# Four reorderings in a two-layer encoder kernel: transposes, operand combinations, a tanh, and a last combination

## The chip, the cores and the metric

The kernel runs on one core of a Trainium2 chip. The metric is the device time of one execution in microseconds, the median of several runs. The names of the engines are those of the profile: PE multiplies matrices, DVE is the vector engine, ACT the scalar engine (copies and activation functions), POOL and SP mainly issue DMAs here.

## What is computed

The reference is an encoder trunk on 512 tokens of width 1024, in float32, with two layers and a final RMSNorm:

```python
for l in range(DEPTH):
    x = x + 0.5 * swiglu(rms_norm(x, ffn1_norm[l]), ffn1_w_in[l], ffn1_w_out[l])
    x = x + mixer(rms_norm(x, mix_norm[l]), ...)
    x = x + 0.5 * swiglu(rms_norm(x, ffn2_norm[l]), ffn2_w_in[l], ffn2_w_out[l])
return rms_norm(x, final_norm)

def mixer(h, w_in, gate_bias, rpb, w_na_out, w_f_out, w_o):
    ...
    y_na = neighbourhood_attention(q, k, v, rpb) @ w_na_out
    y_f = fourier_mix(uf) @ w_f_out
    g_na = jax.nn.sigmoid(ga + gate_bias[0])
    g_f = jax.nn.sigmoid(gf + gate_bias[1])
    return (g_na * y_na + g_f * y_f) @ w_o
```

SwiGLU has width 2816. The weights come from HBM, some blocks more than once; the trace shows 355 MB read.

## The kernel before

**Arithmetic.** Every float32 operand is split into a rounded part hi and a remainder lo; ACT makes hi (L286, or L172 for a negated weight) and DVE makes lo (L287, or L173). A product is then three matmuls, hi·hi, hi·lo and lo·hi (`mm3`, L280 to L282), each 128x128 by 128x512. Activations are the stationary operand, weights the moving one.

**Strassen.** The large matrix products are done on 2x2 blocks in seven products instead of eight. `product` takes one of them: four k-tiles by two token blocks by three matmuls, 24 in all, into a pair of PSUM banks. The operands are blocks of the activations or combinations of them; in the gate blocks t1, t2 and t3 (`minus`, L1078 and L1079, the additions at L1087, then `parts`, which splits them into t1h, t1l and so on). Pair A holds products 1, 6, 7 and 4 in turn, pair B products 5 and 3, pair C product 2. Before a pair gets its next product, `snap` (L436, ACT) copies it out as sn.

**Weights.** `Stream` holds the list of weight granules (128x1024, 512 KB) in the order of use. `ws.next()` hands out the next one and sees to it that two more are split; raw granules are fetched up to eight ahead, by DMAs from SP (L150). Sums of two weight blocks come from additive DMAs that POOL issues (L152 at loading, L179 after a granule has been split) or from DVE (L170). There are three buffers for hi and three for lo of a granule, so the split of one has to wait until the matmuls of the granule three places earlier are through.

**Order.** The kernel is written in a tile framework. The program text gives a priority, and a scheduler plans the queue of each engine, with buffers taken from rotating pools (23 slots of 4 KB per partition in the main one, eight PSUM banks); on the chip each engine then works its queue off. So two instructions of one engine can stand in another order than in the text. `tc.high_priority()` puts the small steps of `rstd` first.

**The places that the change touches.**

- FFN stage (`stage_ffn`): the first 256 columns are done plainly (pairs `pcl`, four banks), then five column blocks `jb` by Strassen. The plain block's gate is tanh (L510, needs `norm.rh` from `rstd`) and two DVE steps per half (L514, L515); its result is transposed by `to_at` (PE L459, ACT L463). The loop's order of products is 1, 5, 6, 2, 7, 3, 4. Behind it come the 21 steps of the output matrix, with `make` for the operand of a step (DVE L546, split into c1h, c1l and so on), three steps for product 4 at the end; c4 is their operand. In the last FFN `finish` multiplies the finished half of x by its rstd and the final gain (L662) and stores it.
- Mixer (`stage_mixer`): after attention and Fourier mixing, `fill(o, ns, 0)` multiplies the attention output by half of `na_w_out` (n: four token blocks of 12 matmuls, copied out at L933 as fs). Then two gate blocks, one for each half of the 1024 channels, with products in the order 1, 5, 2, 6, 7, 3, 4; `after` names functions to call behind a product. Behind the products `less` (L441), `arg` (L944, tanh at L948) and `gated` (L952) make the gates; `both` (L959) adds the two branches. The first block's result `ga0` = fs[0, j], j being the half of the tokens, is transposed by `to_channels` (PE L1023, ACT L1024) into mq, the operand of the output matrix `w`, whose first operands m1 and m5 are read behind the second gate block.
- `squares` (L322): ACT squares x, keeps the row sums, and writes the squares themselves into a scratch tile, junk.

Of the kernel before, what the change touches and what calls it, by code (L numbers as in the profile page):

```python
# [9 lines left out]
F32 = mybir.dt.float32  # L10
F32R = mybir.dt.float32r
BF16 = mybir.dt.bfloat16
I32 = mybir.dt.int32
AF = mybir.ActivationFunctionType
ALU = mybir.AluOpType
AX = mybir.AxisListType

P = 128
D = 1024
T = 512  # L20
# [72 lines left out]
def encoder_kernel(  # L93
# [3 lines left out]
    V, S, G, PE = nc.vector, nc.scalar, nc.gpsimd, nc.tensor  # L97

    cp = ctx.enter_context(tc.tile_pool(name="cp", bufs=1))
    sp = ctx.enter_context(tc.tile_pool(name="sp", bufs=1))  # L100
# [8 lines left out]
    def nm(s):  # L109
        uid[0] += 1  # L110
        return f"{s}_{uid[0]}"

    def slot(dt=F32, s="k", shape=(4, 256)):
        return kp.tile([P, *shape], dt, tag="k", name=nm(s), bufs=23)
# [8 lines left out]
    def pair(s="ps"):  # L123
        return [bank(s), bank(s)]
# [119 lines left out]
    class Stream:  # L244
# [25 lines left out]
        def next(self):  # L270
            self.prep(self.pos + 1 + AHEAD)
            it = self.items[self.pos]
            self.pos += 1
            return it.out

    ws = Stream()
# [29 lines left out]
    class Norm:  # L306
# [10 lines left out]

        def squares(self, i, j):
            for tb in (2 * j, 2 * j + 1):
                junk = sp.tile([P, T], BF16, tag="junk", name=nm("junk"), bufs=1)  # L320
                k = 4 * i + tb
                S.activation(junk, x[:, tb, i * T : (i + 1) * T], AF.Square, accum_out=self.ssq[:, k : k + 1])  # L322

# [102 lines left out]
    def parts(src, s):  # L426
        h, l = slot(F32R, s + "h"), slot(F32R, s + "l")
        split(h, l, src)
        return h, l, 0
# [3 lines left out]
    def snap(ps):  # L433
        t = slot(F32, "sn", (2, T))
        for b in range(2):
            S.activation(t[:, b, :], ps[b], AF.Copy)  # L436
        return t
# [5 lines left out]
    def stage_ffn(norm, nxt, late):  # L443
# [25 lines left out]
        pcl = [pair("cl"), pair("cl")]  # L469
# [20 lines left out]
        for js in ((1,), (0,)):  # L490
# [4 lines left out]
        t1 = combo(b11, b11, b12, ALU.subtract, "t1")  # L495
        t3 = combo(b12, b12, b22, ALU.subtract, "t3")
        t2 = combo(b22, b22, b11, ALU.add, "t2")
# [3 lines left out]
        acts = {  # L501
            1: (hx[0], lx[0], 0), 2: (hx[1], lx[1], 0), 3: (hx[1], lx[1], 256), 4: (hx[0], lx[0], 256),
            5: t1, 6: t2, 7: t3,
        }
        late_at = []
        for j in range(2):
            th = slot(F32, "th", (2, 256))
            for b in range(2):
                c = 2 * j + b
                S.activation(th[:, b, :], pcl[j][b][:, 0:256], AF.Tanh, scale=norm.rh[:, c : c + 1])  # L510
            for b in range(2):
                c = 2 * j + b
                g, u = pcl[j][b][:, 0:256], pcl[j][b][:, 256:512]
                V.scalar_tensor_tensor(th[:, b, :], th[:, b, :], 1.0, g, ALU.add, ALU.mult)  # L514
                V.scalar_tensor_tensor(th[:, b, :], u, norm.r2[:, c : c + 1], th[:, b, :], ALU.mult, ALU.mult)  # L515
            late_at.append((th, j, 0, 2))

        def settle_at():
            while late_at:
                to_at(*late_at.pop(0))  # L520
# [52 lines left out]
        for jb in range(NB):  # L573
            f0 = 2 + 4 * jb
            pa = pair("A")
            product(pa, acts[1], K4, True)
            s1 = snap(pa)
            if jb:
                settle_at()
            pb = pair("B")  # L580
            product(pb, acts[5], K4, True)
            sb = snap(pb)
            settle_at()
            product(pa, acts[6], K4, False, again=True)
            s2 = snap(pa)
            pc = pair("C")
            product(pc, acts[2], K4, True)
            less(pc, s1)
            z1 = gate(s1, 0)
            product(pa, acts[7], K4, False, again=True)  # L590
            less(pa, sb)
            product(pb, acts[3], K4, False, again=True)
            less(pb, s2)
            z2 = gate(s2, 1)
            times(z2, [sb[:, 0, :], sb[:, 1, :]], 1)
            if jb == NB - 1:
                make(0)
                make(1)
            product(pa, acts[4], K4, False, again=True)
            times(z1, pa, 0)  # L600
            late_at += [(z2, 1, f0, 4), (z1, 0, f0, 4)]

        ps = {}
        for i, (m, c, _) in enumerate(steps):
            make(i)
            if i:
                make(i + 1)
            key = {6: 1, 4: 7}.get(m, m)
            if key not in ps:
                ps[key] = pair(f"o{key}")  # L610
            if m == 4 and c == 0 and nxt.mix:
                ws.finish_stage()
                swap_pools(1)
            product(ps[key], made.pop(i), list(range(len(CHUNK[0][c]))), c == 0 and m in (1, 2, 3, 5, 7), c == 2, m in (4, 6))
            if i == 0:
                settle_at()
            make(i + 2)
            if not late:
                if i == 6:
                    nxt.quad(0, 0)  # L620
                elif m == 4 and c == 0:
                    nxt.quad(1, 1)
                    nxt.quad(0, 1)
            if c < 2:
                continue
            if m == 1:
                update(ps[1], 0, 0, -1)
            elif m == 2:
                update(ps[2], 0, 0, 1)
                nxt.squares(0, 0)  # L630
            elif m == 5:
                update(ps[5], 0, 1, 1)
                update(ps[5], 1, 1, -1)
            elif m == 6:
                for q in ((1, 1, 1), (0, 1, -1), (1, 0, 1)):
                    update(ps[1], *q)
            elif m == 7:
                update(ps[7], 1, 1, 1)
                nxt.squares(1, 1)
            elif m == 3:  # L640
                update(ps[3], 0, 1, 1)
                nxt.squares(0, 1)
                if late:
                    finish(nxt, 1)
            else:
                update(ps[7], 1, 0, 1)
                nxt.squares(1, 0)
                if late:
                    finish(nxt, 0)
                else:  # L650
                    nxt.later((1, 0))
# [3 lines left out]
    def finish(norm, j):  # L655
        if gf[0] is None:
            gf[0] = slot(F32, "gf", (D,))
            nc.sync.dma_start(out=gf[0], in_=bass.AP(tensor=gfin.tensor, offset=gfin.offset, ap=[[0, P], [1, D]]))
        r = norm.rstd((j,))
        for b in range(2):  # L660
            o_ = slot(F32, "o", (D,))
            V.scalar_tensor_tensor(o_, x[:, 2 * j + b, :], r[:, b : b + 1], gf[0], ALU.mult, ALU.mult)  # L662
            nc.sync.dma_start(out=out[:, 2 * j + b, :], in_=o_)


    def stage_mixer(l, norm, nxt):
# [140 lines left out]
        o, q, k, bms = [], {}, {}, {}  # L807
# [116 lines left out]
        fs, ns = {}, {}  # L924

        def fill(src, to, i):

            w = [ws.next(), ws.next()]
            for tb in range(TB):
                if tb % 2 == 0:  # L930
                    to[i, tb // 2] = slot(F32, "fs", (2, T))
                ps = rows_of(src, tb, w)
                S.activation(to[i, tb // 2][:, tb % 2, :], ps, AF.Copy)  # L933
                yield
# [81 lines left out]
        def to_channels(i, ga, j):  # L1016
            mq[i, j] = slot(F32, "mq")
            for q in range(2):
                tr = bank("tr").rearrange("p (a b) -> p a b", a=2)
                for k in range(2):  # L1020
                    for b in range(2):
                        d = (2 * q + k) * P
                        PE.transpose(tr[:, k, b * P : (b + 1) * P], ga[j][:, b, d : d + P], ident)  # L1023
                S.activation(mq[i, j][:, 2 * q : 2 * q + 2, :], tr, AF.Copy)  # L1024

        u = proj_U()
# [37 lines left out]
        bias = []  # L1064
# [10 lines left out]
        def minus(p, q, s):  # L1075
            t, u = slot(F32, s), slot(F32, s)
            for z, d in enumerate((t, u)):
                V.tensor_tensor(d, p[z], q[z], ALU.subtract)  # L1078
            V.tensor_tensor(t, t, u, ALU.add)  # L1079
            return t  # L1080

        t12 = minus(B[0, 0], B[0, 1], "t1")
        acts[5] = parts(t12, "t1")
        for _ in fill(o, ns, 0):
            pass
        for z in B[1, 1]:
            V.tensor_tensor(t12, t12, z, ALU.add)  # L1087
        acts[6] = parts(t12, "t2")

        def third():  # L1090
            acts[7] = parts(minus(B[0, 1], B[1, 1], "t3"), "t3")
# [3 lines left out]
            V.tensor_tensor(t12, t12, B[1, 0][1], ALU.add)  # L1095
            split(hx[0][:, :, 256:512], lx[0][:, :, 256:512], t12)

        ga0 = gate_block(0, bias, acts, {2: third, 6: fourth})

        def turn():  # L1100
            for j in range(2):
                to_channels(0, ga0, j)

        ga1 = gate_block(1, bias, acts, {1: turn})
        m00, m01 = mq[0, 0], mq[0, 1]
        a1 = parts(m00, "m1")
        a5 = combo(m00, m00, m01, ALU.subtract, "m5")
# [71 lines left out]
    norm = Norm(0)  # L1179
# [149 lines left out]
```

## Time and profile before

| What | Value |
|---|---|
| Median of 3 runs | 1972.65 us (1972.23 to 1976.64) |
| The profiled execution itself | 1974.07 us |
| Its span, first to last instruction | 1971.8 us |
| Mean granted TensorE clock | 0.992 |
| PE matmuls | 8997 |
| DMA | 361.82 MB, 183 GB/s mean |

Times in the profile count from the start of the span. A row of a timeline has its start, its length, engine, line, operation, output<-inputs, shapes, a count, and in brackets the idle time of the engine before it and what ended that. A row of the stretches has its bounds and length, then busy time and instructions of PE, PEld (weight loads), DVE, ACT and POOL, then the granted clock of PE (1.00 is full speed), the share of the DMA engines' time that was busy, and GB/s. A row of the waits has the waiting instruction, what it waited for, the sum in us, how often, and the longest.

### The profile page before, as it was taken

The page shows a single profiled execution, that of the slowest core. Times are in us where ns is not written, and L with a number is a line of the kernel's source. Part 1 is how long each engine was busy: PE and PEld are TensorE (multiplying, and loading weights), DVE is VectorE, ACT ScalarE, POOL GpSimd, SP SyncE. Part 2 cuts the span into 40 slices and gives each one's busy share as a digit, 9 for nine tenths or more (in the row PEclk, how much of TensorE's full clock was granted, in tenths as well). Part 3 has the DMA queues.
Part 4 walks back from the last instruction along what each step waited for, and adds up shares of the span by engine and source line. Part 5 has one row for each costly group of instructions (what it writes and reads, how often), then busy time and mean ns, then how long its engine had stood idle before and what let it go on. Part 6 is the DMA issues. An engine that isn't in the chain of part 4 may idle for free.

```text
span 1971.8 us, 24577 instructions
## 1 busy us (share of the span) xinstructions
PE 1923.9 (98%) x8997; PEld 1590.0 (81%) x8997; DVE 1617.0 (82%) x1936; ACT 1122.8 (57%) x1594; POOL 199.3 (10%) x242
## 2 busy tenths in 40 slices
PE   8999999999999999999999999999999999999997
PEld 6888887888778888888788888878887788888885
DVE  8777899598779877889977878996878788777897
ACT  6555666445555655566555556653555566555653
POOL 0011011200111000101000100102101110000010
PEclk9999999999999999999999999999999999999999
DMA  8677599221977567749757765974039874775692
GB/s 291 172 193 201 154 250 328 70 67 55 256 194 200 139 185 203 188 151 261 225 139 203 190 171 171 283 254 113 28 116 238 204 192 133 207 180 161 186 282 104
DMA packets 105704, 361.82 MB, mean 183 GB/s; under 512 B 12016, under 2 KB 14192, under 8 KB 105584
## 3 DMA queue, kind: packets, MB, share of 16 engines
q1 hardware_dynamic: 78576, 266.92, 39.8%
q0 software_dynamic: 27008, 93.34, 25.9%
q8 instruction: 70, 1.15, 0.2%
q14 instruction: 50, 0.41, 0.1%
HBM read 354.97 MB, written 2.10 MB: 181 GB/s over the span
## 4 chain that ended last, share of the span: by engine, by line
PE 78%; DVE 12%; issue 3%; DMA 3%; ACT 2%; SPq 0%; DVEq 0%; ACTq 0%
PE A L280 8%; PE A L282 8%; PE A L281 8%; PE o L281 5%; PE o L282 5%; PE o L280 5%; PE B L280 4%; PE B L281 4%; PE B L282 4%; PE ps L281 4%; PE ps L282 4%; PE ps L280 4%; DVE wlo L287 3%; DMA raw<-in_wst_dram 3%; PE C L282 2%
## 5 line engine op out<-in xcount | busy, mean ns | idle before, releaser
L287 DVE TENSOR_TENSOR wlo<-raw,whi 128x1024 fp32r<-128x1024 f32 (+1 forms) x522 | 621.8, 1197 | 275.7 <-ACT whi L286 274.7
L286 ACT ACTIVATE whi<-raw 128x1024 fp32r<-128x1024 f32 (+1 forms) x522 | 540.8, 1038 | 524.2 <-PE A L282 133.2
L152 POOL DMA_DIRECT2D raw<-in_wst_dram x152 | 131.8, 877 | 1369.5 <-DMA raw<-in_wst_dram 861.4
L170 DVE TENSOR_TENSOR raw<-raw,raw 128x1024 f32<-128x1024 f32 (+1 forms) x128 | 151.0, 1189 | 2.4
L281 PE MATMUL A<-wlo,xh 128*128 128x512 f32 x384 | 149.5, 389 | 0.6 <-DVE wlo L173 0.6
L282 PE MATMUL A<-whi,xl 128*128 128x512 f32 x384 | 149.4, 389 | 0.0
L280 PE MATMUL A<-whi,xh 128*128 128x512 f32 x384 | 148.6, 389 | 0.0
L172 ACT ACTIVATE whi<-raw 128x1024 fp32r<-128x1024 f32 x76 | 78.9, 1038 | 86.5 <-PE B L282 33.2
L173 DVE SCALAR_TENSOR_TENSOR wlo<-raw,whi 128x1024 fp32r<-128x1024 f32 x76 | 89.9, 1194 | 22.0 <-ACT whi L172 22.0
L281 PEld LDWEIGHTS A<-wlo,xh 128*128 128x128 f32 x384 | 72.1, 188 | 16.0 <-DVE wlo L173 1.0
L280 PEld LDWEIGHTS A<-whi,xh 128*128 128x128 f32 x384 | 72.1, 188 | 14.9
L282 PEld LDWEIGHTS A<-whi,xl 128*128 128x128 f32 x384 | 72.1, 188 | 14.9
L436 ACT ACTIVATE sn<-A 128x512 f32<-128x512 f32 x96 | 56.9, 598 | 43.3 <-PE A L282 43.3
L280 PE MATMUL A<-whi,t3h 128*128 128x512 f32 x192 | 76.2, 397 | 4.7 <-ACT sn L436 4.7
L280 PE MATMUL A<-whi,t2h 128*128 128x512 f32 x192 | 76.0, 396 | 3.9 <-ACT sn L436 2.7
L280 PE MATMUL B<-whi,t1h 128*128 128x512 f32 x192 | 76.8, 401 | 1.1 <-ACT whi L286 1.1
L281 PE MATMUL A<-wlo,t2h 128*128 128x512 f32 x192 | 75.5, 393 | 1.5 <-DVE wlo L287 1.5
L281 PE MATMUL B<-wlo,t1h 128*128 128x512 f32 x192 | 75.3, 392 | 0.8 <-DVE wlo L287 0.8
L281 PE MATMUL A<-wlo,t3h 128*128 128x512 f32 x192 | 76.1, 396 | 0.0
L282 PE MATMUL A<-whi,t3l 128*128 128x512 f32 x192 | 75.9, 395 | 0.0
L282 PE MATMUL A<-whi,t2l 128*128 128x512 f32 x192 | 75.4, 392 | 0.0
L282 PE MATMUL B<-whi,t1l 128*128 128x512 f32 x192 | 75.1, 391 | 0.0
(336 smaller groups left out, 4930.4 us busy)
## 6 DMA issues: line engine op xcount, KB each, us to landing
raw<-in_wst_dram SPq DMA_DIRECT2D x462, 512.0 KB
raw<-in_wst_dram POOLq DMA_DIRECT2D x168, 512.0 KB, 8.0
raw<-in_wst_dram SPq DMA_DIRECT2D x32, 256.0 KB
vs<-v SPq DMA_DIRECT2D x12, 256.0 KB
bw<-in_rpb_dram SPq DMA_DIRECT2D x32, 68.0 KB
xt<-in_xtr_dram SPq DMA_DIRECT2D x8, 256.0 KB
x<-in_xin_dram SPq DMA_DIRECT2D x4, 512.0 KB
raw<-in_wst_dram POOLq DMA_DIRECT2D x8, 256.0 KB, 9.2
```

The source lines that it names most:

```text
L152: G.dma_start(out=self.t, in_=wst[GRAN_AT[self.plus]][:, 0 : self.n], accum_op=ALU.add)
L170: V.tensor_tensor(t, t, self.add.t, ALU.add)
L172: S.activation(hi, t, AF.Copy, scale=-1.0)
L173: V.scalar_tensor_tensor(lo, t, -1.0, hi.bitcast(F32), ALU.mult, ALU.subtract)
L280: PE.matmul(ps, lh, rh, start=start, stop=False, skip_group_check=again)
L281: PE.matmul(ps, lh, rl, start=False, stop=False, skip_group_check=again)
L282: PE.matmul(ps, ll, rh, start=False, stop=stop, skip_group_check=again)
L286: S.activation(hi, src, AF.Copy)
L287: V.tensor_tensor(lo, src, hi.bitcast(F32), ALU.subtract)
L436: S.activation(t[:, b, :], ps[b], AF.Copy)
```

## The change

- The transposes of `ga0` stood behind product 1 of the second gate block, both halves together (`turn`). Now half j=1 stands behind product 5 and half j=0 behind product 2.
- t1 and t2 of the gate blocks, t2 formerly behind n, are both made ahead of n, in a region that fixes the order of DVE's instructions: the splits of n's two granules and of product 1's first, t1, t2, then what `next(n_fill)` issues on DVE first, the split of product 1's second granule. Other engines are not bound by the region. t3 moves from behind product 2 to behind product 1.
- In the FFN stages with `norm.idx` 0 (the first of the program) the plain block's tanh and DVE steps move from ahead of the loop to behind the copies of products 1 and 5, and its transposes from ahead of product 6 to behind it. In the other FFN stages they stay.
- In the last FFN, `make(i + 3)`, the operand of the very last step, is called ahead of `finish` for half j=1.
- junk gets two buffers instead of one.

```diff
-                junk = sp.tile([P, T], BF16, tag="junk", name=nm("junk"), bufs=1)
+                junk = sp.tile([P, T], BF16, tag="junk", name=nm("junk"), bufs=2)
...
-        for j in range(2):
-            th = slot(F32, "th", (2, 256))
...
-            late_at.append((th, j, 0, 2))
+
+        def plain_out():
+            for j in range(2):
+                th = slot(F32, "th", (2, 256))
...
+                late_at.append((th, j, 0, 2))
+
+        if norm.idx:
+            plain_out()
...
             sb = snap(pb)
-            settle_at()
+            if jb == 0 and norm.idx == 0:
+                plain_out()
+            else:
+                settle_at()
             product(pa, acts[6], K4, False, again=True)
             s2 = snap(pa)
+            settle_at()
...
                 if late:
+                    make(i + 3)
                     finish(nxt, 1)
...
-        t12 = minus(B[0, 0], B[0, 1], "t1")
-        acts[5] = parts(t12, "t1")
-        for _ in fill(o, ns, 0):
+        with tc.manual_schedule(engines={mybir.EngineType.DVE}):
+            ws.prep(ws.pos + 3)
+            t12 = minus(B[0, 0], B[0, 1], "t1")
+            acts[5] = parts(t12, "t1")
+            for z in B[1, 1]:
+                V.tensor_tensor(t12, t12, z, ALU.add)
+            acts[6] = parts(t12, "t2")
+            n_fill = fill(o, ns, 0)
+            next(n_fill)
+        for _ in n_fill:
             pass
-        for z in B[1, 1]:
-            V.tensor_tensor(t12, t12, z, ALU.add)
-        acts[6] = parts(t12, "t2")
...
-        ga0 = gate_block(0, bias, acts, {2: third, 6: fourth})
-
-        def turn():
-            for j in range(2):
-                to_channels(0, ga0, j)
-
-        ga1 = gate_block(1, bias, acts, {1: turn})
+        ga0 = gate_block(0, bias, acts, {1: third, 6: fourth})
+
+        ga1 = gate_block(1, bias, acts, {5: lambda: to_channels(0, ga0, 1), 2: lambda: to_channels(0, ga0, 0)})
```

More of the change, by code (lines that the diff above doesn't have):

```diff
@@ L505, in stage_ffn @@
         late_at = []
-        for j in range(2):
-            th = slot(F32, "th", (2, 256))
[L508 to L515, printed above, removed]
-            late_at.append((th, j, 0, 2))
+        def plain_out():
+            for j in range(2):
+                th = slot(F32, "th", (2, 256))
+                for b in range(2):
+                    c = 2 * j + b
+                    S.activation(th[:, b, :], pcl[j][b][:, 0:256], AF.Tanh, scale=norm.rh[:, c : c + 1])
+                for b in range(2):
+                    c = 2 * j + b
+                    g, u = pcl[j][b][:, 0:256], pcl[j][b][:, 256:512]
+                    V.scalar_tensor_tensor(th[:, b, :], th[:, b, :], 1.0, g, ALU.add, ALU.mult)
+                    V.scalar_tensor_tensor(th[:, b, :], u, norm.r2[:, c : c + 1], th[:, b, :], ALU.mult, ALU.mult)
+                late_at.append((th, j, 0, 2))
+        if norm.idx:
+            plain_out()
         def settle_at():
```

## The prediction

> **What bounds the kernel now.** I read the page, then who PE waits for, then the stretches around the long waits with the granted clock, then single engines there.
>
> ```profile
> span 1971.8 us, 24577 instructions
> ...
> PE 1923.9 (98%) x8997; PEld 1590.0 (81%) x8997; DVE 1617.0 (82%) x1936; ACT 1122.8 (57%) x1594; POOL 199.3 (10%) x242
> ```
> ```profile
> PE tr L1023 <- DVE fs L959: 8.6, 2, 4.5
> PE A L280 <- ACT sn L436: 7.5, 3, 2.7
> PE o L282 <- DVE c4l L287: 4.1, 1, 4.1
> ...
> PE A L281 <- DVE wlo L287: 1.5, 2, 0.8
> ...
> PE A L280 <- ACT whi L286: 1.1, 2, 0.7
> ```
>
> PE is busy 1923.9 of 1971.8 us, so only 47.9 us are idle, and no other engine can gain anything unless PE waits for it. Five rows of its waits hold 22.8 us, and all five stand where the diff edits: L1023 are the moved transposes (once in each of two layers), L436 are the PSUM copies that tanh stands ahead of, c4l is the last combination, and the two short rows are the first gate block. Each place has its stretch:
>
> ```profile
> 43.50:54.50 11.00, 8.26 (x34) 6.56 (x34) 8.50 (x13) 7.89 (x14) 0.00 (x0) 0.84 0.32 105
> 526.00:540.00 14.00, 10.47 (x37) 7.59 (x36) 12.37 (x13) 8.62 (x10) 2.98 (x4) 0.88 0.81 196
> 557.00:567.00 10.00, 5.90 (x28) 4.91 (x27) 4.77 (x5) 4.65 (x7) 1.72 (x2) 0.83 0.86 205
> 1500.00:1514.00 14.00, 10.14 (x36) 7.35 (x35) 11.99 (x13) 8.29 (x10) 2.77 (x4) 0.88 0.79 188
> 1531.00:1541.00 10.00, 5.51 (x28) 4.73 (x27) 5.14 (x5) 4.64 (x7) 1.72 (x2) 0.83 0.95 238
> 1950.00:1960.00 10.00, 5.93 (x20) 4.40 (x19) 4.74 (x10) 0.00 (x0) 0.00 (x0) 0.83 0.26 105
> ```
> ```profile
> 961.00:969.00 8.00, 5.48 (x16) 3.77 (x15) 7.21 (x8) 4.60 (x7) 0.00 (x0) 0.79 0.74 220
> 576.00:596.00 20.00, 20.00 (x90) 16.57 (x89) 16.45 (x20) 10.90 (x12) 2.58 (x3) 1.00 0.92 218
> ```
>
> The second column is PE's busy time, the third from the end the granted clock, the next the DMA share. Two losses can be read off. Idle is length less busy: 2.74, 3.53, 4.10, 3.86, 4.49 and 4.07 us, 22.8 in all. Lost clock is length times (1 − clock): 1.8, 1.7, 1.7, 1.7, 1.7 and 1.7 us, 10.3 in all, because after such a pause matmuls run at a lower clock for a while. So at most about 33 us can be had in the four places. The last row is the undisturbed pace: 90 matmuls in 20 us, 0.22 us each, 5.3 us for a product of 24 and 2.7 for half of one (one weight granule).
>
> [...]
>
> **Part 1, the transposes of the merged half.**
>
> ```profile
> 554.21 1.21 DVE L959 TENSOR_TENSOR fs<-fs,fs 128x1024 f32<-128x1024 f32 x1
> ...
> 556.00 2.35 DVE L287 TENSOR_TENSOR wlo<-raw,whi 128x1024 fp32r<-128x1024 f32 x2
> ...
> 560.55 1.22 DVE L959 TENSOR_TENSOR fs<-fs,fs 128x1024 f32<-128x1024 f32 x1
> ```
>
> All 16 transposes stand behind the first product of the second gate block, which needs 5.3 us, and the half j=0 is added up only at 561.77. Half j=1 is ready at 555.42. After the change PE goes straight into the next product, whose weights are split by 558.35; j=1 is transposed some 5.3 us later and j=0 another 6 us later, both behind their additions. The 16 transposes and four copies (L1024) are the same work. Their readers, the first operands of the output matrix, come five products later. Gone are 4.10 + 1.7 and 4.49 + 1.7 = 12.0 us. What can be late next is a transfer: the DMA shares are 0.86 and 0.95 there. If half comes back as DMA waits it is 6. I take 11.
>
> **Part 2, the gates' combinations.** Of the 3.53 us in layer 0, 1.2 are waits for weights (whi, wlo) and 2.36 for the copy of A behind the sixth product.
>
> ```profile
> 526.48 1.06 ACT L286 ACTIVATE whi<-raw 128x1024 fp32r<-128x1024 f32 x1 [5.87 <-DMA raw<-in_wst_dram]
> 527.44 1.04 ACT L286 ACTIVATE t3h<-t 128x1024 fp32r<-128x1024 f32 x1
> ...
> 531.47 1.06 ACT L948 ACTIVATE sn<-sn 128x1024 f32<-128x1024 f32 x1 [2.04 <-DVE sn L944]
> ...
> 533.38 1.06 ACT L436 ACTIVATE sn<-A 128x512 f32<-128x512 f32 x2
> ```
> ```profile
> 580.47 0.60 ACT L436 ACTIVATE sn<-A 128x512 f32<-128x512 f32 x1
> ```
>
> The second gate block has the same copy at 580.47 and, by its row above, no idle time: one half is copied while PE finishes the other. So 2.36 us are not inherent; the copy is late because t3, less, tanh and a weight copy pile up in front. With t1, t2 and t3 out of the way all 3.53 + 1.7 can go. The price is in the first product:
>
> ```profile
> 506.87 1.06 ACT L172 ACTIVATE whi<-raw 128x1024 fp32r<-128x1024 f32 x1 [7.90 <-issue]
> 508.18 1.06 ACT L286 ACTIVATE whi<-raw 128x1024 fp32r<-128x1024 f32 x1 [0.25 <-PE ps L282]
> 509.15 1.04 ACT L286 ACTIVATE t1h<-t 128x1024 fp32r<-128x1024 f32 x1
> ```
> ```profile
> 502.54 1.22 DVE L1079 TENSOR_TENSOR t<-t,t 128x1024 f32<-128x1024 f32 x1
> 507.96 1.23 DVE L173 SCALAR_TENSOR_TENSOR wlo<-raw,whi 128x1024 fp32r<-128x1024 f32 x1 [4.20 <-ACT whi L172]
> ...
> 512.93 1.23 DVE L1087 TENSOR_TENSOR t<-t,xl 128x1024 f32<-128x1024 f32 x1
> ...
> 516.34 1.22 DVE L287 TENSOR_TENSOR t2l<-t,t2h 128x1024 fp32r<-128x1024 f32 x1
> ```
>
> n's last matmul ends just before 508.18, so the first product starts about 508 and wants the lo half of its second granule (L173, ready at 509.19) at about 510.9. The region on DVE puts that split behind t1l, two additions and t2l. Best: ACT makes t1h at once at 503.76, and 1.04 + 1.22 + 2.46 + 1.04 + 1.22 + 1.23 end at 511.97, a wait of 1.1. Worst: only DVE is pinned, t1h stays behind both weight copies until 510.19, the additions end at 514.16 as now, t2h, t2l and the split end about 517.6, a wait of 6.7. Between them: PE is handed the fifth product's ready half meanwhile and waits about 2. That PE's order is not bound to the code shows here, where transposes that the code names ahead of the product run inside it:
>
> ```profile
> 46.83 0.39 PE L282 MATMUL A<-whi,t2l 128*128 128x512 f32 x1
> 47.06 0.27 PE L459 MATMUL tr<-ident,th 128*128 128x128 f32 x1
> 47.09 0.54 PE L280 MATMUL A<-whi,t2h 128*128 128x512 f32 x1
> ```
>
> Queued behind the waiting DVE are the splits of the fifth product and the additive loads that POOL issues after them. The net of a layer lies between −5.2 + 1.1 = −4.1 and −5.2 + 6.7 + 1.7 = +3.2. I take the middle wait of 2 us and 0.7 for transfers that are late at the quicker pace (share 0.81): −2.5 a layer, −5 in all.
>
> **Part 3, tanh of the first plain block.**
>
> ```profile
> 43.21 1.06 ACT L286 ACTIVATE whi<-raw 128x1024 fp32r<-128x1024 f32 x1 [2.84 <-DVE rh L389]
> 44.17 1.55 ACT L510 ACTIVATE th<-cl,rh 128x256 f32<-128x256 f32 x4
> 45.59 1.10 ACT L436 ACTIVATE sn<-A 128x512 f32<-128x512 f32 x2
> ```
>
> The copies of A need only the first product, but stand behind four tanh that need rstd. Moved in front they fit into ACT's 2.84 us idle ahead of 43.21, and PE need not stop: the gain is up to 2.74 + 1.8 = 4.5. Against it: the four pcl banks stay taken until the tanh and eight DVE steps are through, and the eight transposes and pair C wait for them; they have the sixth product's 5.3 us as cover, and without it the wait just moves, gain 0. I take 3.5. The second junk buffer I cost at nothing: both squares are ACT's own, in order.
>
> **Part 4, the last combination.**
>
> ```profile
> 1948.37 1.04 ACT L286 ACTIVATE c4h<-at 128x1024 fp32r<-128x1024 f32 x1
> ```
> ```profile
> 1951.40 2.48 DVE L662 SCALAR_TENSOR_TENSOR o<-x,r,gf 128x1024 f32<-128x1024 f32 x2
> 1953.79 1.22 DVE L287 TENSOR_TENSOR c4l<-at,c4h 128x1024 fp32r<-128x1024 f32 x1
> ```
>
> c4h is there at 1949.41; c4l waits for the rstd steps and the two output products of 2.48 us. With c4l ahead of the products alone, PE still waits 4.07 − 2.48 = 1.6: gain 2.5, and 4.2 if the clock stays up. Ahead of the rstd steps too, nothing is left: 5.8. The output of half j=1 goes 1.2 us later, still 12 us ahead of the end. I take 4.5.
>
> **Sum.** 11 + 5 + 3.5 + 4.5 = 24 us. The profiled execution took 1974.07 us (span 1971.8, 2.3 around it), 1.4 above the median of 1972.65; the edits take the same from either, so 1972.65 − 24 = about 1949.
>
> **Rivals.** (A) The chain does not do what it says, because ACT's order is not pinned: t1h stays behind the weight copies and the first product waits 6.7 us. For it: the order of the rows 506.87 to 509.15. Against: PE can be given other products. Price +3.2 × 2 instead of −5: 1972.65 − 24 + 11.4 = about 1960. (B) All goes, 12 + 8.2 + 4.5 + 5.8 = 30.5: about 1942. For it: the second gate block runs the same pattern without idle time. Against: DMA share 0.95. (C) Transfers take the place of the waits: half of part 1 comes back and parts 2 and 3 give nothing: 24 − 5 − 5 − 3.5 = 10.5, about 1962. (D) Slower: t2h comes to stand in ACT's queue behind a weight copy that waits for its transfer, as t3h did at 526.48. The split that the first product needs would follow near 530, 19 us late; with 1.7 of clock less 5.2 that is +15.5 a layer, 31 less the other 19: about 1985. It decides from a delay of about 13 us a layer. Against: that copy needs a buffer which the first product still holds.
>
> **How the numbers follow.** Forecast 0.52, A 0.18, B 0.12, C 0.13, D 0.05. A run can tell 0.3%, about 6 us, from no change; forecast, A, B and most of C lie beyond it: faster 0.89, same 0.06, slower 0.05. The range leaves out D and the ends of B and C: 1940 to 1963. The instruction order is planned anew for the whole program, which may move waits elsewhere by a few us (the 2.5 us at 961 occur in one of four such blocks).
>
> **What would show it.** Part 1: no wait on L1023, clock 1.00 there. Part 2: copies of A at the sixth product without PE idle, and a wait for wlo L173 of 1 to 2 us (right) or 6 (A). Part 3: sn ahead of th on ACT. Part 4: c4l ahead of o. Wrong would be new PE waits for raw transfers in the gate blocks.

## The result and the profile after

The changed kernel took 1960.36 us (median of 4 runs, 1957.84 to 1960.91), the one before, in the same sitting, 1974.61 (4 runs). The ratio is 0.9926 with a 95% interval of 0.9909 to 0.9943, that is −14.25 us. The profiled execution took 1960.45 us. The forecast was −24 us to 1949, rival (A) said 1960. In this kernel the moved lines lie 10 lower in the mixer and in the last combination's surroundings (L1023 is L1033, L1087 is L1097, L662 is L672), and the tanh L510 is L512.

The page of the kernel after, span and busy time:

```profile
span 1958.0 us, 24573 instructions
...
PE 1918.9 (98%) x8997; PEld 1585.9 (81%) x8997; DVE 1616.4 (83%) x1936; ACT 1121.0 (57%) x1594; POOL 198.3 (10%) x242
```

Idle time of PE is 1958.0 − 1918.9 = 39.1 us, against 47.9 before. The view of PE's waits in the kernel after tells which are left:

```profile
PE A L281 <- DVE wlo L173: 12.4, 4, 5.7
PE o L281 <- DVE wlo L287: 4.5, 5, 1.6
...
PE A L281 <- DVE wlo L287: 0.5, 1, 0.5
```

The waits of the transposes, of the copies of A and of c4l are gone from the list. A new one heads it: product 1 of the first gate block waits for the split of its second granule, 5.7 us in each layer. The stretches of the kernel after at the same places:

```profile
39.50:50.50 11.00, 10.61 (x49) 8.28 (x49) 10.42 (x18) 8.82 (x16) 0.00 (x0) 1.00 0.53 147
505.00:519.00 14.00, 8.27 (x28) 6.37 (x27) 11.48 (x10) 6.80 (x11) 3.41 (x4) 0.76 0.85 201
528.00:542.00 14.00, 14.00 (x63) 11.37 (x62) 8.77 (x10) 7.11 (x8) 2.61 (x3) 1.00 0.91 226
548.00:572.00 24.00, 23.60 (x111) 19.11 (x110) 19.97 (x23) 14.39 (x18) 4.86 (x6) 1.00 0.97 233
1476.00:1492.00 16.00, 10.27 (x33) 7.88 (x33) 13.19 (x12) 7.79 (x11) 3.41 (x4) 0.79 0.91 222
1518.00:1542.00 24.00, 24.00 (x115) 20.05 (x115) 19.77 (x22) 14.68 (x19) 5.16 (x6) 1.00 0.94 233
1926.00:1942.00 16.00, 14.38 (x61) 11.02 (x60) 15.73 (x24) 10.83 (x17) 0.00 (x0) 1.00 0.00 1
```

Four of the places look as forecast. The first FFN (39.5) is down from 2.74 us idle to 0.39, at full clock. Behind product 6 of the first gate block (528) PE has no idle time. The transposes (548 and 1518) have 0.40 and 0.00 us, at clock 1.00. At the end (1926) 1.62 us are left of 4.07. The two rows of clock 0.76 and 0.79 are new: 14.00 − 8.27 = 5.73 us and 16.00 − 10.27 = 5.73 us of idle time, each with slow matmuls behind it: from 513.60 to 517.20 the granted clock is 0.50, so some 1.8 us are lost beside the 5.73.

Where those come from is shown by ACT's and DVE's timelines of the kernel after, ahead of the first product, which starts at 504.1:

```profile
502.98 1.06 ACT L172 ACTIVATE whi<-raw 128x1024 fp32r<-128x1024 f32 x1 [7.90 <-issue]
504.29 1.06 ACT L286 ACTIVATE whi<-raw 128x1024 fp32r<-128x1024 f32 x1 [0.25 <-PE ps L282]
505.26 1.04 ACT L286 ACTIVATE t1h<-t 128x1024 fp32r<-128x1024 f32 x1
```
```profile
498.65 1.22 DVE L1089 TENSOR_TENSOR t<-t,t 128x1024 f32<-128x1024 f32 x1
506.33 1.23 DVE L287 TENSOR_TENSOR t1l<-t,t1h 128x1024 fp32r<-128x1024 f32 x1 [6.46 <-ACT t1h L286]
...
512.34 1.22 DVE L173 SCALAR_TENSOR_TENSOR wlo<-raw,whi 128x1024 fp32r<-128x1024 f32 x1
```

t is ready at 499.87, but t1h stands behind both weight copies in ACT's queue, as it did before the change. DVE, whose order is now fixed, stands idle for 6.46 us and can't do the split L173 in that time although its input is there at 504.04. Then come t1l, two additions and t2l, and the split ends at 513.56. PE did two matmuls of product 5 in between and no more.

### The profile page after: what moved, and what is told of

The parts are those of the page before. It is cut to its first block, busy times and chain, and to the rows that moved or that the text cites. A ratio compares the mean times of both kernels' runs of the same rounds, so it can differ in the third digit from the quotient of the medians.

```text
span 1958.0 us, 24573 instructions
## 1 busy us (share of the span) xinstructions
PE 1918.9 (98%) x8997; PEld 1585.9 (81%) x8997; DVE 1616.4 (83%) x1936; ACT 1121.0 (57%) x1594; POOL 198.3 (10%) x242
## 4 chain that ended last, share of the span: by engine, by line
PE 83%; DVE 10%; DMA 3%; issue 2%; ACT 2%; SPq 0%; DVEq 0%; POOL 0%; ACTq 0%; POOLq 0%
PE A L281 8%; PE A L282 8%; PE A L280 8%; PE o L281 5%; PE o L282 5%; PE o L280 5%; PE B L281 4%; PE B L282 4%; PE B L280 4%; PE ps L281 4%; PE ps L282 4%; PE ps L280 4%; DVE wlo L287 3%; DMA raw<-in_wst_dram 2%; PE C L281 2%
## 5 line engine op out<-in xcount | busy, mean ns | idle before, releaser
L287 DVE TENSOR_TENSOR wlo<-raw,whi 128x1024 fp32r<-128x1024 f32 (+1 forms) x522 | 620.9, 1196 | 259.2 <-ACT whi L286 258.0
L281 PE MATMUL A<-wlo,xh 128*128 128x512 f32 x384 | 152.0, 396 | 12.9 <-DVE wlo L173 12.4
L173 DVE SCALAR_TENSOR_TENSOR wlo<-raw,whi 128x1024 fp32r<-128x1024 f32 x76 | 89.8, 1193 | 13.5 <-ACT whi L172 13.5
L281 PEld LDWEIGHTS A<-wlo,xh 128*128 128x128 f32 x384 | 73.1, 190 | 30.2 <-DVE wlo L173 14.1
L281 PE MATMUL B<-wlo,t1h 128*128 128x512 f32 x192 | 75.4, 393 | 1.3 <-DVE wlo L287 1.2
L280 PE MATMUL C<-whi,xh 128*128 128x512 f32 x192 | 75.0, 390 | 0.0
L281 PE MATMUL C<-wlo,xh 128*128 128x512 f32 x192 | 74.8, 390 | 0.0
L281 PE MATMUL A<-wlo,t3h 128*128 128x512 f32 x192 | 74.7, 389 | 0.0
L281 PE MATMUL A<-wlo,t2h 128*128 128x512 f32 x192 | 74.7, 389 | 0.0
```

What stands on the lines that cost most here:

```text
L173: V.scalar_tensor_tensor(lo, t, -1.0, hi.bitcast(F32), ALU.mult, ALU.subtract)
L280: PE.matmul(ps, lh, rh, start=start, stop=False, skip_group_check=again)
L281: PE.matmul(ps, lh, rl, start=False, stop=False, skip_group_check=again)
L287: V.tensor_tensor(lo, src, hi.bitcast(F32), ALU.subtract)
```

## The experiments

Each kernel is compared with the one before in the same sitting (1974.61 us for the kernel after, 1975.7 to 1975.9 in the three sittings of the others), so one per mille is 2 us, and kernels of different sittings are compared by their ratios. "From A to wA" is, in a trace, the time from the first matmul of the first gate block to the first matmul of the output matrix, in layer 0 and layer 1: the waits that parts 1 and 2 touch lie inside. It was 100.8 and 101.2 before, and 98.8 and 97.7 after.

| Kernel | Median us | Ratio [95%] | From A to wA |
|---|---|---|---|
| after | 1960.36 | 0.9926 [0.9909, 0.9943] | 98.8, 97.7 |
| e1: after without part 2 | 1953.58 | 0.9887 [0.9873, 0.9900] | 93.8, 95.4 |
| e2: after, ACT's order fixed too | 1951.68 | 0.9876 [0.9860, 0.9891] | 95.1, 93.8 |
| e3: e2 with the split between t1 and t2 | 1952.64 | 0.9883 [0.9869, 0.9897] | 95.3, 94.9 |
| e4: before with part 1 alone | 1962.81 | 0.9935 [0.9922, 0.9948] | 94.5, 96.3 |
| e5: before with part 2 alone | 1976.45 | 1.0005 [0.9997, 1.0014] | 101.7, 103.6 |
| e7: e3 without additive transfers | 1944.41 | 0.9839 [0.9827, 0.9852] | 90.3, 90.3 |
| e8: e1 without additive transfers | 1941.90 | 0.9829 [0.9816, 0.9841] | 89.5, 89.4 |
| e10: e3 with DVE additions instead | 1954.91 | 0.9891 [0.9876, 0.9905] | 97.5, 95.5 |
| e12: e1 with a later t2 | 1954.09 | 0.9902 [0.9884, 0.9920] | 95.3, 95.5 |
| e13: e12 with later transposes of j=0 | 1955.97 | 0.9901 [0.9887, 0.9915] | 96.3, 97.5 |
| e14: before with parts 3 and 4 | 1965.08 | 0.9954 [0.9940, 0.9969] | 100.8, 102.2 |

The theory behind e1 to e3: part 2 costs time because ACT's order is free, and the rest of the change works; with ACT fixed, part 2 would give what was forecast. The rival: the waits that part 2 was to remove have another cause, transfers, and early combinations give nothing.

**e1, part 2 undone.** In the kernel after:

```diff
-        with tc.manual_schedule(engines={mybir.EngineType.DVE}):
-            ws.prep(ws.pos + 3)
-            t12 = minus(B[0, 0], B[0, 1], "t1")
-            acts[5] = parts(t12, "t1")
-            for z in B[1, 1]:
-                V.tensor_tensor(t12, t12, z, ALU.add)
-            acts[6] = parts(t12, "t2")
-            n_fill = fill(o, ns, 0)
-            next(n_fill)
-        for _ in n_fill:
+        t12 = minus(B[0, 0], B[0, 1], "t1")
+        acts[5] = parts(t12, "t1")
+        for _ in fill(o, ns, 0):
             pass
+        for z in B[1, 1]:
+            V.tensor_tensor(t12, t12, z, ALU.add)
+        acts[6] = parts(t12, "t2")
...
-        ga0 = gate_block(0, bias, acts, {1: third, 6: fourth})
+        ga0 = gate_block(0, bias, acts, {2: third, 6: fourth})
```

> The changed kernel with part 2 undone (t1, t2, t3 made where they were before), parts 1, 3 and 4 kept. Theory: the region on DVE costs a layer more than it saves (5.7 us wait for the split of the second granule and 1.7 us of clock, against 3.5 us and 1.7 us saved and some late transfers, about +3 us), so undoing it gains about 6 us on the changed kernel: some 20 us under the kernel before, about 1954 us; no wait at the first product, and the 2.4 us wait for the copy of A is back in each layer. Rival: part 2 brings the 2.5 us a layer that the prediction took, and it is part 1 that brings little because transfers are late: about 9 us under the kernel before, about 1965 us.

It took 0.9887, as the theory said: 22 us less than before, and 0.39% or about 7.7 us less than the whole change. Part 2 makes the kernel slower. In the trace the wait of 5.73 us is gone, and the old ones behind product 6 are back; PE's waits in e1 between 500 and 600:

```profile
PE A L280 <- ACT sn L436: 2.4, 1, 2.4
PE A L281 <- DVE wlo L287: 0.8, 1, 0.8
...
```

**e2 and e3, ACT's order fixed as well**, and in e3 the split of product 1's second granule between t1 and t2:

```diff
-        with tc.manual_schedule(engines={mybir.EngineType.DVE}):
+        with tc.manual_schedule(engines={mybir.EngineType.DVE, mybir.EngineType.Activation}):
             ws.prep(ws.pos + 3)
...
             acts[5] = parts(t12, "t1")
+            ws.prep(ws.pos + 4)
...
-            n_fill = fill(o, ns, 0)
-            next(n_fill)
-        for _ in n_fill:
+        for _ in fill(o, ns, 0):
             pass
```

(The first hunk is e2; e3 has all.)

> The changed kernel with the region on DVE and ACT instead of DVE alone. Theory: the 5.7 us wait comes from t1h standing behind two weight copies in ACT's queue; with ACT in the order of the text, t1h runs right behind the last addition of t1, the chain on DVE ends near 1.1 us after PE wants the split, and 4.6 us of the wait and its 1.7 us of clock go in each layer: about 12.6 us under the changed kernel, about 1948 us. Rival: the chain of five DVE steps and two copies is too long in itself, the wait stays at 4 us or more, and the time at about 1958 us.

> As the one with DVE and ACT in the region, but with the split of the second granule (ws.prep) between t1 and the additions of t2 instead of behind t2, and the n product behind the region. Theory: the split then ends near 509 us in the time of the kernel before, ahead of PE's need at 510.9, so there is no wait at the first product, and t2 and t3 are still early enough for products 6 and 7: about 7.4 us a layer under the changed kernel, about 1946 us. Rival: transfers bound the gate block, the waits come back as waits for raw granules there, and it gains no more than half of it: about 1953 us.

The wait at product 1 fell to 0.71 us in e2, which fixes ACT's order and changes nothing else, and was gone in e3; so ACT's order was its cause. But neither is faster than e1 beyond the intervals (0.9876 and 0.9883 against 0.9887). Other waits came in; in e2 the copy of A behind product 6 still keeps PE waiting for 1.43 us. PE's waits in e3 between 500 and 600:

```profile
PE A L281 <- DVE wlo L287: 2.7, 3, 1.4
PE A L280 <- ACT sn L436: 0.2, 1, 0.2
PE A L281 <- DVE wlo L173: 0.2, 1, 0.2
```

Some 0.5 us of the first row and the last row lie elsewhere. The rest stands at products 6 and 7, where e1 waited 2.4 us for the copy of A: 0.76 at product 6, and 0.24 for the copy and 1.39 for a weight's lo half at product 7. So early combinations did bring the copy forward, but the weights behind them are late, and 2.4 us are still lost there against 3.3 in e1. They also cost clock, which e1's did not (0.83 over the 10 us from 525). That speaks for the rival: without the combinations in the way, something else holds PE at the same place for nearly as long.

**e4 and e14, part 1 alone, and parts 3 and 4 alone**, each in the kernel before with the lines of the change as they stand in the diff.

> The kernel before with part 1 alone (the transposes of the merged half moved). Theory: the wait on L1023 and its clock go in both layers, 5.8 and 6.2 us, nothing takes their place: about 12 us under the kernel before, about 1962.6 us. Rival: transfers or splits of the next product are late at the quicker pace and most of it comes back: 1 to 4 us under the kernel before.

> The kernel before with parts 3 and 4 alone. Theory: 3.6 us in the first FFN stage and 4.2 us at the end, as the positions in the traces say: about 8 us under the kernel before. Rival: the two parts owe some of that to parts 1 and 2, and bring 4 us or less.

Part 1 alone gives 0.65% of 1975.9, 12.8 us, and parts 3 and 4 together 0.46%, 9 us. The sum, 1.11%, is e1's 1.13%: these parts add up. The second junk buffer is in e1 and e14 and not in e4; no run has it alone.

**e5, part 2 alone** in the kernel before.

> The kernel before with part 2 alone (the region on DVE, t1 and t2 in it, t3 behind product 1). Theory: about 3 us a layer dearer, some 6 us over the kernel before, about 1981 us, with the 5.7 us wait at the first product in each layer. Rival: part 2 is worth its 2.5 us a layer by itself and only collides with part 1: 5 us under the kernel before.

Neither number came: 1.0005, no difference. The trace has both halves of it. PE's waits in e5 between 500 and 600:

```profile
PE A L281 <- DVE wlo L173: 5.7, 1, 5.7
PE tr L1023 <- DVE fs L959: 3.1, 1, 3.1
```

The new wait of 5.7 us is there, the waits behind product 6 are gone, and the transposes wait 3.1 instead of 4.1 us. So alone it is paid back, and beside part 1 it is not; more on this below.

**e8 and e7, without the additive transfers.** The next theory: the wait behind product 6 comes from weights. ACT's queue there holds a weight copy whose raw granule is still being summed by an additive DMA that POOL issues (L179), and the copy of A stands behind it. In e1:

```profile
523.70 1.06 ACT L286 ACTIVATE whi<-raw 128x1024 fp32r<-128x1024 f32 x1 [5.65 <-DMA raw<-in_wst_dram]
```

ACT was idle for 5.65 us until that transfer landed. The trace shows that the transfer which ended this idle time is the second of those that POOL issues at L179 (its row stands with e12 below). The kernels leave out those additive transfers in the first gate block, so that two of its products use weights that aren't summed, with late combinations as in e1 (e8) and with early ones as in e3 (e7):

```diff
-                        add(d, then=a.key if dma else None)
+                        add(d, then=a.key if dma and not bare else None)
...
-                        add(d, None if dma else a, then=b.key if dma else None)
+                        add(d, None if dma else a, then=b.key if dma and not bare else None)
...
-                strassen(s, lambda q: "g" + q, i, two, ORDER, True)
+                strassen(s, lambda q: "g" + q, i, two, ORDER, True, i == 0)
```

> As the changed kernel with part 2 undone, and without the additive transfers behind the splits of products 5 and 6 in the first gate block (products 6 and 3 there use the wrong sums). Theory: t3, tanh and the copy of A pile up only because a weight copy in front of them waits for its transfer, so the 2.4 us wait at product 7 goes too though t1 to t3 are as late as before: about 1945 us, the same as with t1 and t2 early. Rival: the combinations themselves are in the way; the 2.4 us wait stays and it is some 5 us slower than with t1 and t2 early, about 1950 us.

> As the kernel with t1, the split, then t2 in a region on DVE and ACT, and without the additive transfers that POOL issues behind the splits of products 5 and 6 in the first gate block of each layer; products 6 and 3 there use the wrong sums of weight blocks (that part of the computation is left out). Theory: what is left of the waits at products 6 and 7 (0.8, 0.2 and 1.4 us a layer, with 1.5 to 2 us of clock) is for these transfers, and goes: about 8 us less than with them, about 1945 us. Rival: the waits are for DVE, which is behind with its own steps, and stay: about 1952 us.

Both took the theory's side, and the late one is no worse: 0.9829 against 0.9839. PE's waits in e8 between 500 and 600 are one row:

```profile
PE A L281 <- DVE wlo L173: 0.2, 1, 0.2
```

and the whole block, of e8 and then of e1, reads so in the view by stretches:

```profile
504.00:594.00 90.00, 89.83 (x404) 73.99 (x403) 81.18 (x85) 55.46 (x66) 12.00 (x14) 1.00 0.87 226
```
```profile
505.00:599.00 94.00, 90.51 (x403) 73.60 (x402) 81.00 (x84) 55.10 (x65) 15.52 (x18) 1.00 0.93 236
```

Four transfers fewer (x14 instead of x18 on POOL), t1 to t3 as late as in the kernel before, and the waits for weights and for the copy of A are gone together. So late combinations alone hold nothing up here: it takes the transfers as well. What e8 doesn't separate is the dependence of the copy on the transfer from the 2 MB that no longer pass the DMA engines.

**e10, the same sums made by DVE** instead of additive DMAs for the first gate block:

```diff
-                strassen(s, lambda q: "g" + q, i, two, ORDER, True)
+                strassen(s, lambda q: "g" + q, i, two, ORDER, i == 1)
```

> As the kernel with t1, the split, then t2 in a region on DVE and ACT, with the sums of weight blocks for products 6 and 3 of the first gate block made by DVE (as the FFN stages do) instead of by additive transfers; everything is computed. Theory: the waits for these transfers go, and four additions of 1.2 us on DVE in each layer stand in its idle time: 4 to 8 us less than with the transfers, about 1946 us. Rival: DVE is late with the added work, or raw granules held longer delay the loads: no gain or worse, 1953 us and more.

0.9891, the rival's side. PE's waits in e10 between 500 and 600:

```profile
PE A L280 <- ACT sn L436: 2.3, 1, 2.3
PE A L281 <- DVE wlo L287: 2.0, 4, 0.7
PE B L281 <- DVE wlo L287: 1.5, 1, 1.5
```

The DMA share of the block is 0.79 (0.92 in e3), and DVE's busy time in it 84.2 us (79.9 in e3); now DVE's splits are late. Either way of making the sums cost about the same here.

**e12 and e13, earlier issue of the transfer.** In e12 t2 is made behind product 1 (in a buffer of its own), so that DVE splits product 5's weights earlier and POOL can issue the additive transfers earlier; e13 also moves the transposes of j=0 behind product 7, since their copies to mq stand ahead of a copy of A on ACT (in e4 that copy waited 1.5 us in layer 1).

```diff
-        for z in B[1, 1]:
-            V.tensor_tensor(t12, t12, z, ALU.add)
-        acts[6] = parts(t12, "t2")
+        t2 = []
+
+        def second():
+            t2.append(slot(F32, "t2"))
+            V.tensor_tensor(t2[0], t12, B[1, 1][0], ALU.add)
+            V.tensor_tensor(t2[0], t2[0], B[1, 1][1], ALU.add)
+            acts[6] = parts(t2[0], "t2")
...
-        ga0 = gate_block(0, bias, acts, {2: third, 6: fourth})
+        ga0 = gate_block(0, bias, acts, {1: second, 2: third, 6: fourth})
...
-        ga1 = gate_block(1, bias, acts, {5: lambda: to_channels(0, ga0, 1), 2: lambda: to_channels(0, ga0, 0)})
+        ga1 = gate_block(1, bias, acts, {5: lambda: to_channels(0, ga0, 1), 7: lambda: to_channels(0, ga0, 0)})
```

(Against e1; the last hunk is e13 alone.)

> The changed kernel with part 2 undone and the opposite of it done: t2 is made behind product 1, in a buffer of its own, so that on DVE the split of product 5's second granule stands ahead of one of t2's two additions. Theory: the additive transfer for product 6 is issued about 1 us earlier, lands 1 us earlier, the waits of 0.2 to 0.3 and 0.8 us at product 6 shrink to about nothing and the 2.4 us wait at product 7, which follows from them, goes at least in part: 2 to 6 us under the kernel without part 2, 1948 to 1951 us. Rival: the landing does not follow the issue, because the DMA engines are full there: no difference, about 1953.5 us.

> As the kernel with t2 behind product 1, and with the transposes of half j=0 behind product 7 instead of product 2 of the second gate block, so that their two copies do not stand on ACT ahead of the copy of A. Theory: the wait for the copy of A in the second gate block (0.35 us without part 2, 1.5 us with part 1 alone, both in layer 1) goes: 0 to 1 us less than with them behind product 2, hardly to be told in the time. Rival: mq comes too late for the output matrix and a wait of more than 1 us appears ahead of it.

No gain: 0.9902 and 0.9901. The wait behind product 6 is still there in e12, in both layers. PE now waits for the weight copy that stands in ACT's queue just ahead of the copy of A, for two matmuls of product 3 that are placed ahead of product 7; PE's waits in e12 between 500 and 600:

```profile
PE B L280 <- ACT whi L286: 3.0, 1, 3.0
PE A L281 <- DVE wlo L287: 0.8, 1, 0.8
```

POOL's second issue of these transfers, in e1 and then in e12:

```profile
513.03 0.85 POOL L179 DMA_DIRECT2D raw<-in_wst_dram  x1 [3.06 <-DVE wlo L287]
```
```profile
510.06 0.85 POOL L179 DMA_DIRECT2D raw<-in_wst_dram  x1 [2.10 <-DVE wlo L287]
```

The first gate block starts at 505.43 in e1 and at 503.41 in e12, so the issue moved from 7.60 to 6.65 us behind its start, 0.95 us earlier. The transfer landed 18.17 and 18.06 us behind the start, 0.11 earlier (18.28 and 17.95 in layer 1). The kernel after shows the same the other way round: there it was issued 12.27 us behind the start, 4.66 later than in e1, and landed 19.06 behind it, 0.9 later. In e12 (and e1) the DMA engines were full then, share 1.04 (1.05 in e1):

```profile
500.00:520.00 20.00, 20.00 (x90) 16.57 (x89) 14.08 (x12) 12.04 (x16) 4.28 (x5) 1.00 1.04 281
```

e13's own theory fell as well: the copy of A in the second gate block still kept PE waiting, 0.87 us in layer 0 and 1.19 in layer 1, which is more than e12's nothing and 0.38. Why, I did not settle.

## Why the prediction was right or wrong

The total came out 9.4 us short of the forecast's −23.7 (1949 against 1972.65) and within its range. That hides two errors of opposite sign: parts 1, 3 and 4 gave about 22 us (e1) against 19, and part 2 cost 7.7 us (after against e1; the interval of that difference is some ±4) instead of giving 5. That the total fell inside the range is partly luck.

- **Part 1 right.** Forecast 11, at most 12.0; measured 12.8 (e4, 0.9922 to 0.9948, so 10 to 15). No wait on the transposes, clock 1.00. The transfers that were to bring half of it back did not.
- **Part 3 right.** sn stands ahead of th on ACT. The first matmul of n begins 3.9 us earlier in the kernel after (493.2 instead of 497.1), 3.7 on average over the ten traces with this part (1.8 to 4.9); forecast 3.5. ACT's timeline of the kernel after:

```profile
36.41 0.58 ACT L436 ACTIVATE sn<-A 128x512 f32<-128x512 f32 x1
...
39.82 0.58 ACT L436 ACTIVATE sn<-A 128x512 f32<-128x512 f32 x1
...
42.70 0.60 ACT L436 ACTIVATE sn<-B 128x512 f32<-128x512 f32 x1 [1.35 <-PE B L282]
...
45.42 0.83 ACT L512 ACTIVATE th<-cl,rh 128x256 f32<-128x256 f32 x2
```

- **Part 4 right.** From the first A of the last FFN to the last matmul it takes 308.9 us instead of 313.0; 4.1 against a forecast of 4.5. On DVE, in the kernel after, c4l is ahead of both output products:

```profile
1935.62 1.22 DVE L287 TENSOR_TENSOR wlo<-raw,whi 128x1024 fp32r<-128x1024 f32 x1
...
1938.03 1.22 DVE L287 TENSOR_TENSOR c4l<-at,c4h 128x1024 fp32r<-128x1024 f32 x1
...
1943.15 2.48 DVE L672 SCALAR_TENSOR_TENSOR o<-x,r,gf 128x1024 f32<-128x1024 f32 x2
```

The 1.6 us left are a wait for a weight's lo half, as the row "PE o L281 <- DVE wlo L287" above shows, at clock 1.00. Parts 3 and 4 together are 9 us by e14, 8 forecast.

- **Part 2 wrong, in two steps.** The first is "Between them: PE is handed the fifth product's ready half meanwhile and waits about 2", from which came "I take the middle wait of 2 us". The rows 506.87 to 509.15 of the prediction showed ACT's order, nothing in the change touched it, and PE was handed two matmuls. The wait was 5.73 us, near the worst case of 6.7 that rival (A) had priced, and the half clock behind it cost some 1.8 us more. e2 shows that this order was the cause. The second is "the copy is late because t3, less, tanh and a weight copy pile up in front. With t1, t2 and t3 out of the way all 3.53 + 1.7 can go". The row 526.48 that stood beside it has what came first in its bracket: 5.87 us of idle ACT, ended by a DMA. The pile formed because ACT had been waiting for that transfer. e8 shows it (the waits go with the transfers, the combinations as late as ever), and e7 beside e8 that early combinations then give nothing. With the transfers in place e3 shows that early combinations bring the copy forward, and that a wait for a weight's lo half takes the place of most of it. In the kernel after, those waits are gone for a reason that gives nothing: PE arrives there 5.73 us and some 1.8 us of clock later, and the transfers have landed: the second came 17.9 to 19.1 us behind the block's start in every kernel here that has it.

So rival (A) is what happened, and its 1960 is what was measured, but partly by luck: parts 1, 3 and 4 gave 3 us more than it took them to give, and part 2 cost 7.7 instead of 6.4. Rival (C) had the transfers take back half of part 1 and all of part 3, which they did not; that they leave part 2 without a gain is what e3, e7 and e8 show. (B) would have needed part 2's gain. (D) did not occur: t2h ran at 510.11, ahead of any copy that waits for a transfer.

**What stays open.** Part 2 costs nothing alone that can be told from none (1 us by e5's ratio) and 7.7 us beside the others. By the traces from A to wA it is +0.9 and +2.4 us alone (e5 less before) and +5.0 and +2.3 beside the others (after less e1), so the difference, 4.1 us, is in layer 0. By the view by stretches over the same bounds, part 2 adds 3.2 us of idle time and 1.8 us of busy time (slower matmuls) there beside the others, and alone 1.2 us of idle time and −0.3 us of busy time. Three terms are at hand. Alone, it makes the transposes wait about 1 us less (4.10 to 3.1), which beside part 1 is worth nothing; the kernel after has two further waits of 0.5 and 0.3 us for weights' lo halves that e5 doesn't have; and before had 1.7 us of lost clock behind product 6 that e5 doesn't have, while e1 lost none there (below). That is 3.5 of 4.1 us, argued from single traces and not shown by a run. It also stays open whether the copy of A could be placed ahead of the tanh in ACT's queue, and what that would give: no run tried it.

## What to carry to other kernels

When one engine's order is fixed by hand, check that every input that another engine makes for it is fixed too, or comes from far ahead: here a queue that was left free kept a 1 us copy in its old place, and the fixed engine carried that delay to the next one. Before moving work out of the way of a late instruction, read what ended the idle time ahead of the pile: where that is a transfer, clearing the work behind it may give nothing, as here. And four edits in one change should be priced and tried one by one; three of these gave 22 us, and the fourth took a third of it back.

## What the runs showed of the hardware

**The same pauses cost clock in one run and none in another.** In the prediction's row of 961 to 969 PE is idle 2.52 us at a clock of 0.79. e1 has the same stretch, with the same idle time, 10 us earlier, and e1's and e4's stretches behind product 6 have idle times of 3.31 and 3.13 us. e1, then e4:

```profile
951.00:959.00 8.00, 5.48 (x23) 3.91 (x22) 8.00 (x10) 5.53 (x8) 0.00 (x0) 1.00 0.63 206
523.00:537.00 14.00, 10.69 (x45) 7.99 (x44) 12.12 (x13) 8.41 (x10) 2.62 (x3) 1.00 0.81 185
```
```profile
526.50:540.50 14.00, 10.87 (x39) 7.95 (x38) 12.39 (x13) 8.69 (x10) 2.97 (x4) 0.88 0.84 196
```

1.00 in e1, 0.79 before and 0.88 in e4, where 14 × 0.12 = 1.7 us of clock are lost. The pauses are of about the same length and in the same place of the program, so length alone does not decide. e3 lost as much with 1.63 us of idle time, in two pauses:

```profile
525.00:535.00 10.00, 8.37 (x29) 6.21 (x28) 9.84 (x11) 5.08 (x6) 0.56 (x1) 0.83 1.03 265
```

What decides was not shown: no run here moved a pause by a known time to test it. The prediction's "after such a pause matmuls run at a lower clock for a while" is true of all six of its rows (0.83 to 0.88) and of neither stretch of e1. Nor did it take a pause of more than 2.4 us: the longest in e1's and in e4's stretch behind product 6 is 2.37 us, and the prediction's own 3.53 and 3.86 us around products 6 and 7 are sums of three pauses of at most 2.37. As an estimate from these traces, idle time of 1.6 (e3) to 3.9 us (before) in a stretch cost its length plus nothing (e1) or plus about 1.7 us (before, e3, e4).

**A transfer that was issued earlier hardly landed earlier** when the DMA engines were full: 0.95 us earlier on POOL, 0.11 us earlier at the end (e12 against e1, at a DMA share of 1.04). The rest of the traces agree: issues of this transfer from 6.05 us (e3) to 12.27 us (after) behind the block's start landed between 17.9 and 19.1 us behind it. So in this block moving the issue by a few microseconds was worth almost nothing.
